# Moving the SBUF tiles of a float32r block kernel to addresses that are multiples of 512 bytes

## The chip, the core and the metric

The kernel runs on one core of a Trainium2 chip. The metric is the device time of one execution in microseconds (us). The numbers below come from three timed runs of the kernel before and from one further execution that was recorded with the hardware profiler.

## What is computed

One layer of a block over 2048 positions of width 1024, all in float32. Cut to what matters:

```python
h = rms_norm(x, norm_mix_g)
z = h @ w_in                                  # 1024 -> 2568 columns
u_a, v_a = gelu(z[:512]), gelu(z[512:1024])   # group A: gated heads over blocks of 128 positions
q, k, v, f_logit = the rest of z              # group B: 8 heads of 64, causal attention with a forget gate
out_a = u_a * (masked w_s @ layer_norm(v_a) + b_s)
out_b = softmax(q k^T / 8 + c[t] - c[s]) v    # c = cumsum(log_sigmoid(f_logit + f_bias)), s <= t
x = x + concat(out_a, out_b) @ w_out
a = rms_norm(x, norm_ffn_g) @ w_up            # 1024 -> 2 * 2816, then a causal convolution of width 3
x = x + (silu(gate) * value) @ w_down         # 2816 -> 1024
out = rms_norm(x, norm_final_g)
```

## The kernel before

**Three matmuls for one.** Each float32 operand of a large product is split into a high and a low part of type float32r, and each product is made of three matmuls: high by high, high by low, low by high (`mm3`, lines 208 to 212; `prod`, 1154 to 1156; `mms`, 1356). Nearly all matmuls have a 128x128 stationary operand and a moving operand of 512 columns, which is 2048 bytes in each partition.

**Stages, in order of time.** The input projections for keys, queries, values and the gated heads (`phase_a`, to about 590 us); the output projection of the first half of the tokens (`c_half`); the up-projection and convolution of the first half (`d_half`, from about 720 us to 1470 us); the output projection of the second half (`c_late`); its up-projection, done with seven half-size products instead of eight (`late_half`, `up_mms`); and the down-projection, done in the same way (`down`, from about 1990 us).

**What sets the order.** From about 120 us to 1490 us attention runs as a filler between the matmuls of the other stages: `tick` counts matmuls and calls `step`, which takes the next piece of the generator `b_stream`. A piece of `b_max` (lines 750 and 751) is one block of scores for the row maxima, a piece of `b_mix` has the scores again, transposed (811, 812), and the products with the values (799, 800). The matmul of line 750 uses 96 partitions, all others use 128. A scheduler then orders the instructions of each engine.

**Where tiles lie.** [...] The first pool, `const` (lines 215 to 225), holds the identity that transposes use, `mhalf`, `cols` and `halo`, and ends at byte 3872, which is 7 x 512 + 288. All pools of the left side follow, and since the tiles that large matmuls read have sizes that are multiples of 512 bytes, each of them begins at 288 bytes past a multiple of 512: `whi`, `wlo`, `thi`, `tlo`, `m1`, `t1`, `m2`, `t2`, `v`, `ph`, `pl`, `xh`, `xl`, `wh`, `wl` and the parts of the late stages. On the right side lies attention's pool `bpool`, opened by `b_open` and filled by `b_consts` (masks) and `b_max` (small statistics). To its left, from about 970 us to 1490 us, lies `bxpool`, opened in `d_half` (line 958 and after), from which `room` takes spare buffers for attention; their names have a plus: `e+`, `m2+`, `ph+`, `pl+`, `v+`. They begin at 96 bytes past a multiple of 512. In the built program 320 matmuls read a `+` tile as the moving or as the stationary operand.

**Small rings that the change touches.** `a_layernorm` takes three 64-byte tiles `lns` a call and `a_forget` takes eight 128-byte tiles `fs` a call (function `turn`, lines 597 to 613); `BUFS` says how many buffers each ring has.

Of the kernel before, what the change touches and what calls it, by code (L numbers as in the profile page):

```python
# [8 lines left out]
F32 = mybir.dt.float32  # L9
F32R = mybir.dt.float32r  # L10
BF16 = mybir.dt.bfloat16
AF = mybir.ActivationFunctionType
# [6 lines left out]
P = 128  # L19
# [19 lines left out]

BUFS = {  # L40
    "raw": 2, "rawl": 3, "whi": 5, "wlo": 5, "thi": 2, "tlo": 2, "acc": 4,
# [11 lines left out]
def f32(ap):  # L53
    return ap.bitcast(F32)
# [26 lines left out]
class Block:  # L81
# [134 lines left out]
    def constants(self):  # L216
        nc, a, tc = self.nc, self.a, self.tc
        cp = self.cpool = self.ctx.enter_context(tc.tile_pool(name="const", bufs=1))
        self.ident = cp.tile([P, P], F32, name="ident")
        make_identity(nc, self.ident)  # L220
        self.mhalf = cp.tile([P, 8], F32, name="mhalf")
        nc.gpsimd.memset(self.mhalf, -0.5)
        self.cols = cp.tile([P, 200], F32, name="cols")
        self.halo = cp.tile([P, 2 * NF, 2], F32, name="halo")
        nc.gpsimd.memset(self.halo, 0.0)
        dp = self.ctx.enter_context(tc.tile_pool(name="dram", bufs=1, space=DRAM))
        self.ones_d = dp.tile([2, HALF], F32, name="ones_d")
        t = lambda n, k, s: [dp.tile(s, F32, name=f"{n}{i}") for i in range(k)]
        self.qx = t("qx", 2, [8, 128, HALF])
        self.kx = t("kx", 2, [8, 132, HALF])  # L230
        self.cc = t("cc", 2, [8, 2, HALF])
        self.vd = t("vd", 2, [HALF, 8, P])
        self.mixh = t("mixh", 4, [D, TB])
        self.mixl = t("mixl", 4, [D, TB])
        self.rows_d = [t(f"rows{i}_", 8, [P, D]) for i in range(2)]
        self.act_d = [t(f"act{i}_", NF, [P, HALF]) for i in range(2)]
        self.tw_d = t("tw", NF // 2, [P, 2, D])
# [342 lines left out]
    def a_forget(self, half, b):  # L580

        nc, sp, pp = self.nc, self.sp, self.ap
        hT = self.hT[b]
        pl = self.til(pp, [16, TB], F32, "mm" if half else "tp")
        for k in range(KC):
            nc.tensor.matmul(pl, lhsT=self.wf[:, k, :], rhs=hT[0][:, k, :], start=k == 0, stop=False)
            self.tick()
            nc.tensor.matmul(pl, lhsT=self.wf[:, k, :], rhs=hT[1][:, k, :], start=False, stop=k == KC - 1)
            self.tick()
        lg = self.til(sp, [16, TB], F32, "ln")  # L590
        nc.scalar.activation(lg, pl, AF.Copy)

        def turn():
            pt = self.til(pp, [P, 4, 16], F32, "tp")
            for i in range(4):
                nc.tensor.transpose(pt[:, i, :], lg[:, i * P:(i + 1) * P], self.ident[:16, :16])
            t = lambda: self.til(sp, [P, 4, 8], F32, "fs")
            z0, z = t(), t()
            nc.vector.tensor_copy(z0, pt[:, :, 8:16])
            nc.vector.tensor_tensor(z, pt[:, :, 0:8], z0, op=ALU.add)  # L600
            nc.vector.tensor_tensor(z, z, self.scales[half][b].unsqueeze(2).broadcast_to([P, 4, 8]), op=ALU.mult)
            nc.vector.tensor_tensor(z, z, self.fb.unsqueeze(1).broadcast_to([P, 4, 8]), op=ALU.add)

            az, e, u, d, ru, lu = t(), t(), t(), t(), t(), t()
            nc.scalar.activation(az, z, AF.Abs)
            nc.scalar.activation(e, az, AF.Exp, scale=-1.0)
            nc.vector.tensor_scalar(u, e, 1.0, None, ALU.add)
            nc.vector.scalar_tensor_tensor(d, u, -1.0, e, op0=ALU.add, op1=ALU.subtract)
            nc.vector.reciprocal(ru, u)
            nc.vector.tensor_tensor(d, d, ru, op=ALU.mult)  # L610
            nc.scalar.activation(lu, u, AF.Ln)
            nc.vector.tensor_tensor(lu, lu, d, op=ALU.subtract)
            nc.vector.scalar_tensor_tensor(lu, z, 0.0, lu, op0=ALU.min, op1=ALU.subtract)
            lh = self.til(sp, [P, 4, 8], F32R, "fr")
            ll = self.til(sp, [P, 4, 8], F32R, "fr")
            nc.vector.tensor_copy(lh, lu)
            nc.vector.tensor_tensor(ll, lu, f32(lh), op=ALU.subtract)
            self.defer(70, lambda: cumulate(lh, ll))

        def cumulate(lh, ll):  # L620
            pc = self.til(pp, [8, TB], F32, "tp")
            for i in range(4):
                w, o = self.tri[:, 0:TB - P * i], pc[:, P * i:]
                nc.tensor.matmul(o, lhsT=lh[:, i, :], rhs=w, start=i == 0, stop=False)
                nc.tensor.matmul(o, lhsT=ll[:, i, :], rhs=w, start=False, stop=i == 3)
            c = self.til(sp, [8, TB], F32, "ln")
            nc.vector.tensor_scalar(c, pc, self.carry, None, ALU.add)
            nc.vector.tensor_copy(self.carry, c[:, TB - 1:TB])
            for sc, dst in ((-1.0, self.cc[half]), (1.0, self.kx[half][:, 130:132, :])):
                hl = self.til(sp, [8, 2, TB], F32R, "vn")  # L630
                rh, rl = hl[:, 0, :], hl[:, 1, :]
                nc.scalar.activation(rh, c, AF.Copy, scale=sc)
                nc.vector.scalar_tensor_tensor(rl, c, sc, f32(rh), op0=ALU.mult, op1=ALU.subtract)
                self.dma(dst[:, 0, b * TB:(b + 1) * TB], f32(rh))
                self.dma(dst[:, 1, b * TB:(b + 1) * TB], f32(rl))

        self.defer(12, turn)


# [10 lines left out]
    def b_consts(self):  # L650
        nc, bp = self.nc, self.bp
        ones = self.til(self.sp, [P, TB], F32, "st")[:2, :]
        nc.gpsimd.memset(ones, 1.0)
        for i in range(2):
            self.dma(self.ones_d[:, i * TB:(i + 1) * TB], ones)
        for k in self.kx:
            self.dma(k[:, 128:130, :], self.ones_d.unsqueeze(0).broadcast_to([8, 2, HALF]))
        self.mask = bp.tile([P, TB], BF16, name="mask")
        nc.gpsimd.memset(self.mask, 0.0)

        nc.gpsimd.affine_select(out=self.mask, in_=self.mask, compare_op=ALU.is_ge, fill=BIG, base=384,
                                pattern=[[-1, TB]], channel_multiplier=1)

        self.maskT = bp.tile([P, P], BF16, name="maskT")
        nc.gpsimd.memset(self.maskT, 0.0)
        nc.gpsimd.affine_select(out=self.maskT, in_=self.maskT, compare_op=ALU.is_ge, fill=BIG, base=0,
                                pattern=[[1, P]], channel_multiplier=-1)

        self.rowsel = bp.tile([8, 4, P], BF16, name="rowsel")
        nc.gpsimd.memset(self.rowsel, 1.0)  # L670
        for base, mult in ((0, 1), (1, -1)):
            nc.gpsimd.affine_select(out=self.rowsel, in_=self.rowsel, compare_op=ALU.is_ge, fill=0.0, base=base,
                                    pattern=[[-2 * mult, 4], [0, P]], channel_multiplier=mult)
        self.M1, self.T1 = [[self.til(self.mp, [P, TB], F32R, tag) for _ in range(2)] for tag in ("m1", "t1")]
        for m in self.M1:
            nc.gpsimd.memset(f32(m[64:128, :]), 0.0)
            nc.gpsimd.memset(f32(m[96:104, :]), 1.0)
        for t in self.T1:
            nc.gpsimd.memset(f32(t[64:128, :]), 0.0)
            self.dma(f32(t[66:68, :]), self.ones_d[:, 0:TB])  # L680
# [835 lines left out]
```

## Time and profile before

| | before |
|---|---|
| median of 3 runs | 2429.42 us (2428.42 to 2429.88) |
| the profiled execution, its own time | 2425.31 us |
| its span, first to last instruction | 2423.6 us |
| TensorE (PE) busy | 2404.0 us, 99% |
| weight loads (PEld) busy | 1981.1 us, 82% |
| VectorE (DVE) busy | 1755.0 us, 72% |
| ScalarE (ACT) busy | 1352.4 us, 56% |
| GpSimd (POOL) busy | 315.8 us, 13% |
| granted TensorE clock, mean | 0.999 |

In the rows of the profile, PE is a matmul and PEld a weight load. A row of groups names the line of the kernel, the engine, the operation, output<-inputs, sizes and the count, then the busy time in us and the mean duration in ns, then idle time of the engine ahead of them. A row of the timeline begins with the start and the length in us. Matmuls overlap in the pipeline: the recorded length of one of 512 columns is 0.39 us, but the next one starts about 0.23 us after it, so the cost of a matmul is the distance between two starts, and a longer recorded length shows a longer distance.

### The profile page before, as it was taken

What the parts mean: (1) busy time and instruction counts of PE and PEld (TensorE: products, weight loads), DVE (VectorE), ACT (ScalarE), POOL (GpSimd) and SP (SyncE); (2) the same over time, 40 slices, a digit from 0 to 9 for tenths busy, and PEclk for the clock granted to TensorE, in tenths of its full rate; (3) what the DMA queues carried; (4) which work ended last, traced back from release to release, by engine and by line L of the source; (5) the groups of instructions that cost most, each with busy time, mean ns of one, the idle gap of its engine ahead of it and who ended that gap; (6) DMA issues with size and microseconds to landing.
All of it is one profiled execution on the core that took longest, in us unless ns stands there. A gap on an engine that the chain in (4) does not pass through costs nothing.

```text
span 2423.6 us, 32604 instructions
## 1 busy us (share of the span) xinstructions
PE 2404.0 (99%) x10984; PEld 1981.1 (82%) x10984; DVE 1755.0 (72%) x3086; ACT 1352.4 (56%) x2635; POOL 315.8 (13%) x303
## 2 busy tenths in 40 slices
PE   9999999999999999999999999999999999999998
PEld 7788888788788888888888888888888888888887
DVE  5448785565568778878778775598888877957776
ACT  4347766554446555766776764365555455454443
POOL 3114140000241221111012101100000000000000
PEclk9999999999999999999999999999999999999999
DMA  8854636658855444555445565312222238538633
GB/s 291 276 142 120 202 114 178 170 169 265 261 188 183 160 163 161 163 170 181 149 154 180 165 190 199 130 52 88 86 79 87 85 95 306 164 99 296 207 118 122
DMA packets 245031, 400.51 MB, mean 165 GB/s; under 512 B 51240, under 2 KB 109736, under 8 KB 243440
## 3 DMA queue, kind: packets, MB, share of 16 engines
q1 hardware_dynamic: 239824, 374.31, 48.7%
q0 software_dynamic: 5040, 24.12, 2.6%
q8 instruction: 87, 1.43, 0.2%
q14 instruction: 80, 0.66, 0.1%
HBM read 304.76 MB, written 93.72 MB: 164 GB/s over the span
## 4 chain that ended last, share of the span: by engine, by line
PE 68%; DMA 2%; DVE 2%; ACT 1%; issue 1%; POOL 0%; SPq 0%; DVEq 0%; POOLq 0%; ACTq 0%
PE D L1356 14%; PE mm L212 8%; PE mm L208 8%; PE mm L210 8%; PE A L1154 3%; PE A L1156 3%; PE A L1155 3%; PE o L800 2%; PE o L799 2%; PE B L1156 2%; PE B L1155 2%; PE B L1154 2%; PE s L751 1%; PE s L750 1%; PE s L812 1%; PE s L811 1%
## 5 line engine op out<-in xcount | busy, mean ns | idle before, releaser
L210 PE MATMUL mm<-tlo,whi 128*128 128x512 f32 x912 | 358.3, 393 | 0.0
L212 PE MATMUL mm<-thi,wlo 128*128 128x512 f32 x912 | 357.5, 392 | 0.0
L208 PE MATMUL mm<-thi,whi 128*128 128x512 f32 x912 | 357.2, 392 | 0.0
L150 POOL TENSOR_SCALAR whi<-raw 128x1024 fp32r<-128x1024 f32 (+1 forms) x112 | 128.2, 1146 | 980.5 <-PE mm L210 576.5
L208 PE MATMUL mm<-whi,thi 128*128 128x512 f32 x640 | 252.0, 395 | 0.7 <-POOL whi L150 0.7
L212 PE MATMUL mm<-whi,tlo 128*128 128x512 f32 x640 | 251.5, 394 | 1.1 <-DMA tlo<-mixl 1.1
L210 PE MATMUL mm<-wlo,thi 128*128 128x512 f32 x640 | 251.1, 393 | 0.2
L759 ACT ACTIVATE s<-s,part 128x512 f32<-128x512 f32 (+3 forms) x261 | 154.6, 592 | 141.8 <-DVE part L754 85.2
L823 DVE TENSOR_TENSOR pl<-e,ph 128x512 fp32r<-128x512 f32 (+1 forms) x218 | 146.6, 681 | 76.0 <-ACT ph L822 42.4
L208 PEld LDWEIGHTS mm<-thi,whi 128*128 128x128 f32 x912 | 171.4, 188 | 35.9
L212 PEld LDWEIGHTS mm<-thi,wlo 128*128 128x128 f32 x912 | 171.5, 188 | 34.9
L210 PEld LDWEIGHTS mm<-tlo,whi 128*128 128x128 f32 x912 | 171.5, 188 | 34.9
L817 ACT ACTIVATE e<-s 128x512 f32<-128x512 f32 (+1 forms) x222 | 113.8, 529 | 109.5 <-DVE s L815 49.5
L162 DVE TENSOR_TENSOR wlo<-raw,whi 128x1024 fp32r<-128x1024 f32 x104 | 135.6, 1304 | 51.0 <-POOL whi L150 50.8
L822 ACT ACTIVATE ph<-e 128x512 fp32r<-128x512 f32 (+1 forms) x218 | 120.1, 563 | 43.6 <-PE o L799 41.1
L1356 PE MATMUL D<-wl,xh 128*128 128x512 f32 x368 | 141.4, 389 | 0.0
L1356 PE MATMUL D<-wh,xh 128*128 128x512 f32 x368 | 140.8, 389 | 0.2 <-DVE xo L1434 0.2
L212 PEld LDWEIGHTS mm<-whi,tlo 128*128 128x128 f32 x640 | 120.3, 188 | 24.7 <-DMA tlo<-mixl 1.4
L208 PEld LDWEIGHTS mm<-whi,thi 128*128 128x128 f32 x640 | 120.3, 188 | 24.3 <-POOL whi L150 1.0
L210 PEld LDWEIGHTS mm<-wlo,thi 128*128 128x128 f32 x640 | 120.3, 188 | 24.1 <-DVE wlo L162 1.0
L1356 PE MATMUL D<-wh,xl 128*128 128x512 f32 x368 | 137.2, 389 | 0.0
L754 DVE TENSOR_REDUCE part<-s 128x1 f32<-128x512 f32 x149 | 98.5, 683 | 26.6 <-PE s L751 25.9
(1860 smaller groups left out, 5834.8 us busy)
## 6 DMA issues: line engine op xcount, KB each, us to landing
raw<-in_w_up_dram SPq DMA_DIRECT2D x72, 512.0 KB
m<-kx SPq DMA_DIRECT2D x134, 256.0 KB
m<-kx SPq DMA_DIRECT2D x160, 136.0 KB
x<-act SPq DMA_DIRECT2D x84, 256.0 KB
raw<-in_w_in_dram SPq DMA_DIRECT2D x36, 512.0 KB
v<-vd SPq DMA_DIRECT2D x67, 256.0 KB
raw<-in_w_out_dram SPq DMA_DIRECT2D x24, 512.0 KB
tw<-in_w_down_dram SPq DMA_DIRECT2D x11, 1024.0 KB
```

The source lines that it names most:

```text
L150: self.cast_ins = self.nc.gpsimd.tensor_scalar(out, in_, 1.0, 0.0, ALU.mult, ALU.add).ins
L162: nc.vector.tensor_tensor(lo, raw, f32(hi), op=ALU.subtract)
L208: mm(ps, lhsT=ah[k], rhs=bh[k], start=k == 0, stop=False)
L210: mm(ps, lhsT=ah[k], rhs=bl[k], start=False, stop=False)
L212: self.last_mm = mm(ps, lhsT=al[k], rhs=bh[k], start=False, stop=k == n - 1).ins
L759: nc.scalar.activation(ps[:, :n], ps[:, :n], AF.Exp, scale=-1.0, bias=dst, accum_out=ls[:, tt, sb:sb + 1])
L822: nc.scalar.activation(ph[:, c], e[:, c], AF.Copy)
L823: nc.vector.tensor_tensor(pl[:, c], e[:, c], f32(ph[:, c]), op=ALU.subtract)
L1154: mm(ps, lhsT=xh[:, ks], rhs=yh[:, k, :], start=fresh and k == 0, stop=False, **kw)
L1155: mm(ps, lhsT=xh[:, ks], rhs=yl[:, k, :], start=False, stop=False, **kw)
L1156: mm(ps, lhsT=xl[:, ks], rhs=yh[:, k, :], start=False, stop=k == 3, **kw)
L1356: nc.tensor.matmul(bank[t], lhsT=x[i][:, ts], rhs=w[k], start=fresh and j == 0 and i + k == 0, stop=last and i == 1, **kw)
```

## The change

An unused tile of 224 bytes in a partition is put at the end of the `const` pool, and one of 96 bytes behind `maskT` in attention's pool. Everything in the left pools moves up by 224 bytes, so that the tiles that were at 288 are now at a multiple of 512; the tiles of `bxpool` move down by 96 bytes, from 96 past a multiple to a multiple. To make room, the ring `lns` has 8 buffers instead of 9 and the ring `fs` 7 instead of 9, and `a_forget` takes seven tiles a call: the absolute value and the exponential are written in place.

```diff
-    "x": 4, "st": 4, "ln": 2, "vn": 4, "u": 2, "lns": 9, "fs": 9, "fr": 3,
+    "x": 4, "st": 4, "ln": 2, "vn": 4, "u": 2, "lns": 8, "fs": 7, "fr": 3,
...
         self.halo = cp.tile([P, 2 * NF, 2], F32, name="halo")
+        cp.tile([P, 56], F32, name="even")
...
-            az, e, u, d, ru, lu = t(), t(), t(), t(), t(), t()
-            nc.scalar.activation(az, z, AF.Abs)
-            nc.scalar.activation(e, az, AF.Exp, scale=-1.0)
+            e, u, d, ru, lu = t(), t(), t(), t(), t()
+            nc.scalar.activation(e, z, AF.Abs)
+            nc.scalar.activation(e, e, AF.Exp, scale=-1.0)
...
         self.maskT = bp.tile([P, P], BF16, name="maskT")
+        bp.tile([P, 24], F32, name="even")
```

Not all that matmuls read comes to a multiple of 512. The identity stays at 128 past one, the ring `e` of attention (written and read by ScalarE and VectorE, not by matmuls) stays at 288, `tri` (moving operand of 32 matmuls in `cumulate`, lines 624 and 625) moves from 448 to 160, and `sw` (stationary in `a_mixed`) from 480 to 448. The sequence of instructions on each of the five engines is the same in both programs apart from the names of buffers; six instructions of GpSimd (three of line 570, three of line 150) differ in whether they also wait for an earlier instruction of GpSimd itself.

## The prediction

> **What bounds the kernel now.** I read the page first: the span and the engines' busy time, then the chain that ended last by engine.
>
> ```profile
> span 2423.6 us, 32604 instructions
> PE 2404.0 (99%) x10984; PEld 1981.1 (82%) x10984; DVE 1755.0 (72%) x3086; ACT 1352.4 (56%) x2635; POOL 315.8 (13%) x303
> PE 68%; DMA 2%; DVE 2%; ACT 1%; issue 1%; POOL 0%; SPq 0%; DVEq 0%; POOLq 0%; ACTq 0%
> ```
>
> TensorE is busy all the time and no other engine is near it. Only the distance between two matmul starts can move the end, by each matmul's own share. Next I read those distances. First the stretch of the second half's up-projection (busy time by windows; columns: length, PE busy and number of matmuls, clock, DMA), with three rows of its timeline:
>
> ```profile
> 1600.00:1990.00 390.00, 390.00 (x1722) 1.00 0.25 83
> ...
> 1700.17 0.39 PE L1155 MATMUL A<-tlo,xsP3h 128*128 128x512 f32 x1
> 1700.40 0.39 PE L1156 MATMUL A<-tlo,xsP3l 128*128 128x512 f32 x1
> 1700.62 0.39 PE L1154 MATMUL A<-tlo,xsP3h 128*128 128x512 f32 x1
> ```
>
> 390 us for 1722 matmuls of 512 columns is 226.5 ns each, without variation. All these operands lie at 288 past a multiple of 512. I call this the steady spacing. Then the groups, where the recorded length tells the spacing: 389 ns in the late stages, more in the early ones, where attention runs between (last columns: busy us, mean ns of one).
>
> ```profile
> L1356 PE MATMUL D<-wl,xh 128*128 128x512 f32 x368 | 141.4, 389 | 0.0
> ...
> L210 PE MATMUL mm<-tlo,whi 128*128 128x512 f32 x912 | 358.3, 393 | 0.0
> L212 PE MATMUL mm<-thi,wlo 128*128 128x512 f32 x912 | 357.5, 392 | 0.0
> L208 PE MATMUL mm<-thi,whi 128*128 128x512 f32 x912 | 357.2, 392 | 0.0
> L208 PE MATMUL mm<-whi,thi 128*128 128x512 f32 x640 | 252.0, 395 | 0.7 <-POOL whi L150 0.7
> L212 PE MATMUL mm<-whi,tlo 128*128 128x512 f32 x640 | 251.5, 394 | 1.1 <-DMA tlo<-mixl 1.1
> L210 PE MATMUL mm<-wlo,thi 128*128 128x512 f32 x640 | 251.1, 393 | 0.2
> ...
> L750 PE MATMUL s<-m,t 96*128 96x512 f32 x178 | 68.4, 403 | 1.9 <-DMA t<-qx 1.2 <-DMA t<-cc 0.7
> L751 PE MATMUL s<-m,t 128*128 128x512 f32 x157 | 59.2, 401 | 0.0
> ```
>
> So there are two losses to look at: the excess over the steady spacing in the early stages, and the steady spacing itself.
>
> **What starts an excess.** The timeline shows the steady stream broken by a matmul that differs from the one before it. Here it is one with 96 partitions (its sizes begin with 96):
>
> ```profile
> 1009.09 0.39 PE L208 MATMUL mm<-thi,whi 128*128 128x512 f32 x1
> 1009.32 0.40 PE L750 MATMUL s<-m,t 96*128 96x512 f32 x1
> 1009.55 0.40 PE L751 MATMUL s<-m,t 128*128 128x512 f32 x1
> 1009.79 0.40 PE L210 MATMUL mm<-tlo,whi 128*128 128x512 f32 x1
> ```
>
> And here two that read `+` tiles, at 96 past a multiple of 512 between tiles at 288:
>
> ```profile
> 1126.27 0.40 PE L799 MATMUL o<-ph+_2355_10034,v 128*128 128x512 f32 x1
> 1126.51 0.40 PE L208 MATMUL mm<-thi,whi 128*128 128x512 f32 x1
> 1126.75 0.39 PE L800 MATMUL o<-pl+_2356_10035,v 128*128 128x512 f32 x1
> 1126.98 0.39 PE L210 MATMUL mm<-tlo,whi 128*128 128x512 f32 x1
> ...
> 1127.91 0.39 PE L212 MATMUL mm<-thi,wlo 128*128 128x512 f32 x1
> ```
>
> From the first of these rows to the last there are seven spacings in 1.64 us, 234 ns each. So a start that differs from its neighbours' does cost something: about 8 ns on the matmul and on a few behind it.
>
> **The change part by part.** The order of instructions stays, so every term is a duration.
>
> *The `+` tiles come to the same start as the rest.* This is the term that I count on. 320 matmuls read a `+` tile. The lower bound is 0: in that stage matmuls with 96 partitions and transposes break the stream as well, and followers may pay on their account anyway. The upper bound is the whole run above: seven spacings of 234 against 226.5 are 53 ns for two such matmuls, 26 ns each, times 320 is 8.4 us. I take one excess of 7.5 ns for each, 320 x 7.5 = 2.4 us, because the rows with 96 partitions show the same excess right beside them, and what a follower pays is then no longer the tile's doing. [...]
>
> *All other tiles go from 288 to 0 together.* Their starts relative to each other stay as they are. The steady spacing is the same whichever of the tiles is read, and the one float32r operand that starts elsewhere and is not a `+` tile, `tri` at 448 (a multiple of 64), shows no better one:
>
> ```profile
> 492.59 0.40 PE L624 MATMUL tp<-tri,fr 128*8 128x512 f32 x1
> 492.82 0.39 PE L625 MATMUL tp<-tri,fr 128*8 128x512 f32 x1
> 493.05 0.22 PE L811 MATMUL s<-t,m 128*128 128x128 f32 x1
> ```
>
> Two spacings of 0.23 us. I take 0 for this term; what it would be otherwise is the first rival.
>
> *Smaller rings.* The next user of `fs` comes long after the last reader, 59.37 against 72.85 us, and with 8 buffers of `lns` the third call's last tile (written from 205.67 us) takes the one that the first call read last at 174.87 us:
>
> ```profile
> 59.19 0.18 DVE L617 TENSOR_TENSOR fr<-fs,fr 128x32 fp32r<-128x32 f32 x1
> 72.85 0.18 DVE L599 COPY fs<-tp 128x32 f32<-128x32 f32 x1
> ...
> 173.65 1.22 DVE L562 TENSOR_TENSOR ln<-ln,lns 128x1024 f32<-128x1024 f32 x1
> ...
> 205.67 2.90 POOL L570 TENSOR_TENSOR lns<-lns,mhalf 128x16 f32<-128x16 f32 x1 [7.14 <-PE s L784]
> ```
>
> Covers of 13 and 31 us, cost 0; without the cover, a wait of the small chain in `a_forget`, whose product is used 70 matmuls later. Three more casts on GpSimd wait for an earlier instruction of GpSimd, which runs in order anyway: 0. *VectorE, ScalarE and DMA* also see other starts. VectorE is busy for 72% and ScalarE for 56% of the span, and 2%, 1% and 2% of the chain that ended last are VectorE, ScalarE and DMA, so a few per cent of one of them is under 1 us: 0.
>
> The sum: the profiled execution took 2425.3 us (span 2423.6 and 1.7 around it), minus 2.4 is 2422.9. It was 4.1 us faster than the median of the runs shown, so the median to expect is 2429.4 - 2.4 = 2427.0 us, 0.1% less. A measurement of this kernel can tell about 0.2%, or 4.9 us, from no change, so this is no change.
>
> **The rivals.**
>
> *First: the steady spacing is itself a loss from the start at 288, and goes.* For it speak two kinds of short matmul, four transposes that read the identity (at 128 past a multiple of 512) and twelve rows of the gate's products that read `vn` (at 288):
>
> ```profile
> 236.58 0.60 PE L183 MATMUL tp<-ident,u 128*128 128x128 f32 x4
> ...
> 225.16 1.50 PE L524 MATMUL tp<-vn,sw 128*128 128x128 f32 x12
> ...
> L524 PE MATMUL tp<-vn,sw 128*128 128x128 f32 x128 | 18.3, 275 | 0.0
> L183 PE MATMUL tp<-ident,u 128*128 128x128 f32 x64 | 10.3, 272 | 0.0
> ```
>
> Their spacings are (0.60 - 0.272)/3 = 109 and (1.50 - 0.275)/11 = 111.4 ns: with 288 it is 1.9% slower. On 2404 us of TensorE that is 46 us, and the time 2383. Against it: `tri`, and that `vn` is read in two pieces there and the identity in one. [...] Chance 0.14.
>
> *Second: every excess of the early stages goes,* because a stream that starts on a multiple of 512 finds its steady spacing again at once. From the groups: 912 x (4 + 3 + 3) + 640 x (6 + 5 + 4) ns are 18.7 us, 178 x 14 + 157 x 12 another 4.4, together 23 us; the recorded means contain true waits too, so I take 14, and 2415 us. Against it: 96 partitions and transposes still break the stream. Chance 0.16.
>
> *Third, slower: the steady spacing is a property of the start 288 and does not hold at 0.* Place: the late stages from 1570 us, which hold it now. Price: there are (2420 - 1570)/0.2265 = 3750 matmuls; with the 6 ns that the `whi` rows have over 389 it is 22 us, hence 2449 us. It decides from 1200 matmuls on (the 2.4 us gained and 4.9 more, at 6 ns). For it speaks only that a change of start is seen at all; against it, that the steady spacing is the same for all tiles and whatever the other engines do. Chance 0.08.
>
> **How the numbers follow.** Forecast 0.62: 2427.0 us, on its own 2421 (the upper bound of the first term) to 2432. Faster by over 0.2% are the first two rivals, 0.30; slower the third, 0.08; within 0.2% 0.62. The range of 8 in 10 takes the second rival in, with the upper bound of the first term against its middle value, to 2411, and a quarter of the third, to 2436; outside lie the first rival, 0.14, and most of the third, 0.06.
>
> **What would show it.** Right: the window 1600 to 1990 again holds about 1722 matmuls, and rows around a `+` tile start 0.23 us apart, while those of line 750 stay at 0.40 us. Wrong: 389 ns in the late groups gives way to another number (first or third rival), or the `mm` groups fall to 389 in the early stages (second).

## The result, and the profile after

| | before | after |
|---|---|---|
| median of 7 runs each, in turn on one chip | 2429.42 us (2427.00 to 2430.46) | 2421.35 us (2419.37 to 2422.35) |
| ratio after to before, 95% interval | | 0.997 (0.9959 to 0.9980) |
| the profiled execution, its own time | 2425.31 us | 2421.7 us |

By the medians the change makes the kernel 8.1 us faster, 0.33%; by the ratio it is 0.30%. The predicted 2427.0 us has the right sign and the range holds the result, but the likeliest case, "within 0.2%", did not come: a gain of 2.4 us was forecast. The two profiled executions differ by only 3.6 us. So there were two things to find out: where the other 5 us come from, and why the profiles show only part of the gain.

The page of the changed kernel, its span, the busy times, and the chain that ended last by engine:

```profile
span 2420.0 us, 32601 instructions
PE 2401.1 (99%) x10984; PEld 1980.9 (82%) x10984; DVE 1757.0 (73%) x3086; ACT 1352.3 (56%) x2635; POOL 315.2 (13%) x303
PE 93%; DMA 2%; DVE 2%; ACT 1%; issue 1%; POOL 0%; SPq 0%; DVEq 0%; POOLq 0%; ACTq 0%
```

VectorE and ScalarE do their work in the same time as before (1755.0 and 1352.4 us).

TensorE's share of the chain, 93% against 68%, is not more work (busy for 2401.1 against 2404.0 us). The shares of the kernel before add up to 74% only, because its chain can be followed back no further than to a wait of TensorE for `op`:

```profile
632.20 0.61 DVE op L835
632.85 0.50 PE o L799
```

The chain of the changed kernel goes back to the first transfers. This wait is the last of three that are told of below.

The late up-projection, by windows as before (length, PE busy and matmuls, weight loads, the other engines, clock, share of the DMA engines, GB/s):

```profile
1600.00:1990.00 390.00, 390.00 (x1723) 322.92 (x1722) 330.48 (x414) 203.02 (x308) 0.59 (x1) 1.00 0.25 83
```

1723 matmuls against 1722: the steady spacing did not move. Nor did the short matmuls that read `vn`, which begins on a multiple of 512 now; twelve of them take 1.50 us as before:

```profile
224.90 1.50 PE L525 MATMUL tp<-vn,sw 128*128 128x128 f32 x12
```

The timeline around two matmuls that read `+` tiles, and around one with 96 partitions (lines 752 and 753 here are 750 and 751 before):

```profile
1124.15 0.39 PE L801 MATMUL o<-ph+_2351_10032,v 128*128 128x512 f32 x1
1124.38 0.39 PE L208 MATMUL mm<-thi,whi 128*128 128x512 f32 x1
1124.60 0.39 PE L802 MATMUL o<-pl+_2352_10033,v 128*128 128x512 f32 x1
1124.83 0.39 PE L210 MATMUL mm<-tlo,whi 128*128 128x512 f32 x1
...
1125.74 0.39 PE L212 MATMUL mm<-thi,wlo 128*128 128x512 f32 x1
```

```profile
1007.62 0.40 PE L752 MATMUL s<-m,t 96*128 96x512 f32 x1
1007.85 0.40 PE L753 MATMUL s<-m,t 128*128 128x512 f32 x1
1008.09 0.40 PE L210 MATMUL mm<-tlo,whi 128*128 128x512 f32 x1
```

Seven spacings from the first `+` row to the last take 1.59 us, 227 ns each; before they took 1.64 us. All rows there are back at 0.39 us. The rows with 96 partitions stay at 0.40 us. In the groups, the `mm` rows that run beside attention moved by 0 to 1 ns and did not reach 389:

```profile
L210 PE MATMUL mm<-tlo,whi 128*128 128x512 f32 x912 | 357.9, 392 | 0.0
L208 PE MATMUL mm<-thi,whi 128*128 128x512 f32 x912 | 356.8, 391 | 0.0
...
L752 PE MATMUL s<-m,t 96*128 96x512 f32 x178 | 68.3, 403 | 1.6 <-DMA t<-qx 0.9 <-DMA t<-cc 0.5 <-issue 0.2
```

To add up small differences I took the distance from each matmul's start to the next one's, and from it the steady spacing of its width (226.67 ns for 512 columns). What is left I call **excess** when it is up to 20 ns, and a **long wait** at those matmuls where at least one kernel has over 120 ns (what lies between differs little). Summed over the kernel, the excess fell from 15.8 to 12.9 us, so 2.9 us, near the forecast; the long waits were 9.8 us and 9.2 us. The size of the fall is known to some tenths: over matmuls of 256 and more columns alone it is 2.4 us. Counted so, the stretch from 970 to 1490 us, where `+` tiles are read, has 7.3 us of excess before and 4.6 after, and in every other stage the two kernels agree within 0.1 us. The rest of the gain is not in these two traces.

### The profile page after: what moved, and what is told of

The parts are those of the page before. It is cut to its first block, busy times and chain, and to the rows that moved or that the text cites. A ratio compares the mean times of both kernels' runs of the same rounds, so it can differ in the third digit from the quotient of the medians.

```text
span 2420.0 us, 32601 instructions
## 1 busy us (share of the span) xinstructions
PE 2401.1 (99%) x10984; PEld 1980.9 (82%) x10984; DVE 1757.0 (73%) x3086; ACT 1352.3 (56%) x2635; POOL 315.2 (13%) x303
## 4 chain that ended last, share of the span: by engine, by line
PE 93%; DMA 2%; DVE 2%; ACT 1%; issue 1%; POOL 0%; SPq 0%; DVEq 0%; POOLq 0%; ACTq 0%
PE D L1358 15%; PE mm L212 14%; PE mm L210 14%; PE mm L208 14%; PE A L1156 3%; PE A L1157 3%; PE A L1158 3%; PE o L802 2%; PE o L801 2%; PE s L753 2%; PE s L752 2%; PE s L814 2%; PE s L813 2%; PE B L1157 2%; PE B L1158 2%; PE B L1156 2%
```

## The experiments

Two theories stood at the start. Theory R: only a difference of start between neighbouring matmuls' operands costs time. Theory A: a start on a multiple of 512 is itself what helps. A third, N, was that the first profile of before was a lucky execution. The numbers of all kernels are in one table, worked out from the traces: the start of left tiles that matmuls read and of `+` tiles, modulo 512; the sum of excess and of long waits in us; of these the three waits between 627 and 634 us, which are told of below; the share of 2048-byte DMA packets that took over 100 ns between 640 and 950 us; and the time against the kernel before, timed in turn on the same chip (its medians there: 2427.79, 2427.68 and 2428.56 us). The ratio compares runs taken in turn; it differs from the quotient of the two medians by up to 0.07%.

```
kernel    left  +    excess  long   near   packets  median   ratio (95% interval)
                             waits  628    >100 ns
before    288   96   15.8     9.8   1.7    0.20     2429.42
before2   288   96   15.6    13.5   2.2    0.19     2428.42  1.0005 (0.9996 to 1.0014)
rings     288   96   15.7    12.9   1.6    0.19     2427.30  1.0001 (0.9992 to 1.0009)
right     288    0   15.4    11.7   1.7    0.19     2427.11  0.9999 (0.9990 to 1.0008)
left        0   96   15.6     7.5   0.0    0.13     2423.34  0.9984 (0.9975 to 0.9993)
match288  288  288   13.1    12.3   2.0    0.18     2425.07  0.9986 (0.9977 to 0.9995)
all64      64   64   13.5     9.4   0.7    0.18     2425.14  0.9990 (0.9981 to 0.9998)
after       0    0   12.9     9.2   0.0    0.14     2421.35  0.9970 (0.9959 to 0.9980)
after2      0    0   12.8     7.4   0.0    0.14     2420.37  0.9977 (0.9966 to 0.9987)
k128        0    0    9.0    13.2   1.4    0.13     2418.08  0.9962 (0.9949 to 0.9976)
raw0      288   96   15.1     9.3   1.3    0.17     2425.85  0.9991 (0.9982 to 1.0000)
raw288      0    0   13.5     6.5   0.0    0.11     2420.43  0.9971 (0.9960 to 0.9982)
plus352   288  352   15.7    12.1   2.0    0.19     one run
plus32    288   32   13.0     8.4   1.9    0.19     one run
```

The waits are distances from start to start, and so a little longer than the idle times in the rows below. In `match288` and `all64`, 1.4 and 1.6 us are left out of them that lie in stretches with a lower granted clock (mean 0.75 from 664.5 to 668.5 us, and 0.60 from 8 to 11 us). Edits are shown against the changed kernel. The expectations for `right` and `all64` speak of a theory D, which came from the first four experiments and is told further below.

**The kernel before, once more** (`before2`, as it was).

> The kernel before, unchanged, for a second profile and more times. In the two traces so far the spans differ by 3.6 us, the medians by 8.1: the profiled execution of before (2425.3 us) lies below all of its timed runs (2427.0 to 2430.5). Theory R (a mismatch of start between the operands of neighbouring matmuls costs time, nothing else in this change does): the span of this second profile lies near 2424 again and the small excess of matmuls over their steady spacing sums to about 16 us again; then 4 us of the gain lie in something that comes and goes from run to run. Theory N (the first profile of before was lucky): the span comes out at 2426 to 2429 us, and the added time shows as waits for transfers or as more excess. Time against the kernel before: ratio 1.000.

The page's span, and the waits of TensorE between 600 and 640 us (us in total, times, longest):

```profile
span 2427.5 us, 32604 instructions
```

```profile
PE mm L208 <- POOL whi L150: 1.1, 1, 1.1
PE o L799 <- DVE op L835: 0.6, 1, 0.6
PE s L812 <- DMA m<-kx: 0.2, 1, 0.2
```

The span is 3.9 us longer than in the first profile of before; the excess is the same (15.6 us) and the long waits are 3.7 us more. Theory N held: the first profiled execution had fewer waits than most, which is also why it lay 4.1 us under the median.

**The smaller rings alone** (`rings`).

```diff
-        cp.tile([P, 56], F32, name="even")
...
-        bp.tile([P, 24], F32, name="even")
```

> Only the smaller rings of lns and fs and the absolute value and exponential in place; all tiles keep the starts of before (288, and 96 for the + tiles). Theory R and theory A (a start on a multiple of 512 is itself what helps) both: 2429 us, ratio 1.000. Rival: the waits that went near 630 us in the changed kernel went because of the rings and not because of the starts; then about 1.5 us less than before, and the 0.65 us wait for the cast at 627.8 us is absent from this trace too.

Ratio 1.0001, and the waits near 628 us are there (1.6 us). The rings cost and bring nothing that shows here.

**One of the two spaces alone** (`left`: only the one behind the constants; `right`: only the one in attention's pool).

```diff
-        bp.tile([P, 24], F32, name="even")
```

> The rings and the space behind the constants, but none in attention's pool: all tiles that the stationary side reads start at 0, the + tiles stay at 96, so the mismatch between neighbours stays (96 against 0). Theory R: as before, 2427 to 2430 us, ratio 0.999 to 1.000; matmuls with + tiles keep a mean excess of about 5 ns. Theory A: most of the gain is there, 2422 to 2424, ratio 0.997 to 0.998.

```diff
-        cp.tile([P, 56], F32, name="even")
```

> Only the space in attention's pool (and the rings): + tiles at 0, all tiles of the left side at 288 as before. Theory D: the starts still differ and the transfers are those of before, so 2427 to 2428 us, ratio 0.9995 to 1.000; the excess of matmuls with + tiles stays at about 5 ns, the waits near 628 us are there. Theory A (a start on a multiple of 512 is what helps a matmul): the excess of the + tiles falls, 2425, ratio 0.999.

Neither theory was right on `left`. Its excess is that of before (15.6 us; matmuls with `ph+` and `v` keep 6.4 ns against 6.6), as theory R says, and still it gains 0.16%. `right` gains nothing (0.9999; excess 15.4 us): bringing `+` tiles to a multiple of 512 did not help them while the others were at 288.

**Equal starts that are no multiples of 512** (`match288`, `all64`).

```diff
-        cp.tile([P, 56], F32, name="even")
...
-        bp.tile([P, 24], F32, name="even")
+        bp.tile([P, 80], F32, name="even")
```

> The rings, no space behind the constants, and 80 numbers (320 bytes) of space in attention's pool: all tiles start at 288 past a multiple of 512, the + tiles too; nothing starts on a multiple of 512. Theory R: as fast as the changed kernel, 2421 to 2422 us, ratio 0.997; the excess of matmuls with + tiles falls to 0 to 1.5 ns. Theory A: 2427 to 2430 us, ratio 0.999 to 1.000.

```diff
-        cp.tile([P, 56], F32, name="even")
+        cp.tile([P, 72], F32, name="even")
...
-        bp.tile([P, 24], F32, name="even")
+        bp.tile([P, 8], F32, name="even")
```

> All tiles, the + tiles too, start at 64 past a multiple of 512. Equal starts: by theory D the excess is 12.9 to 13.1 us in all, as in the changed kernel. For the transfers it tells whether a multiple of 64 bytes is enough: if so 2421 us, ratio 0.997, no waits near 628 us and packets as short as in the changed kernel (a mean of 28.1 ns for 512 bytes against 29.0); if it takes a multiple of 512, 2424 to 2425 us, ratio 0.9986, and the waits are there.

The timeline of `match288`, then of `left`, at the same matmuls:

```profile
1129.44 0.39 PE L800 MATMUL o<-ph+_2351_10031,v 128*128 128x512 f32 x1
1129.67 0.39 PE L208 MATMUL mm<-thi,whi 128*128 128x512 f32 x1
1129.90 0.39 PE L801 MATMUL o<-pl+_2352_10032,v 128*128 128x512 f32 x1
...
1131.03 0.39 PE L212 MATMUL mm<-thi,wlo 128*128 128x512 f32 x1
```

```profile
1123.20 0.40 PE L800 MATMUL o<-ph+_2351_10031,v 128*128 128x512 f32 x1
1123.43 0.39 PE L208 MATMUL mm<-thi,whi 128*128 128x512 f32 x1
1123.66 0.40 PE L801 MATMUL o<-pl+_2352_10032,v 128*128 128x512 f32 x1
...
1124.82 0.40 PE L212 MATMUL mm<-thi,wlo 128*128 128x512 f32 x1
```

1.59 us at 288 and 288, 1.62 us at 0 and 96. So the matmuls' part goes by theory R: equal starts were enough here, at 0 or at 288. It is worth 2.4 to 2.9 us of excess, and `match288` measures 0.14%; that it would have the whole gain, 0.997, as theory R said, was wrong. The other part comes with the left side's start, 0.16% in `left`. The two add up to the changed kernel's 0.30%, each known to about 0.1%.

`all64` lies between: 0.9990. Its excess, 13.5 us, is a little more than expected (matmuls with `ph+` and `v` keep 2.3 ns, against 1.5 in `match288`). Of the three waits near 628 us one is left (0.7 us), and long packets are nearly as frequent as at 288 (0.18).

**What the left side's start brings.** In the table it is the long waits: the seven kernels with those tiles at 288 (without `raw0`, below) have 8.4 to 13.5 us, mean 11.5, and the four at 0 (without `k128`) 6.5 to 9.2, mean 7.6. Single executions vary by 2 to 3 us, but three waits do not: they are there in all with tiles at 288, `raw0` too, and in none of these four. Of the difference of 3.9 us between the means, 2.1 lie between 600 and 640 us, in these three waits and in small ones just ahead of them. The rest is spread over later waits, in which kernels with equal starts differ among themselves by more than that. GpSimd's casts of the weights show what they wait for (start and length; in brackets idle time and what ended it), here in `before2` and then in the changed kernel:

```profile
617.19 1.41 POOL L150 TENSOR_SCALAR whi<-raw 128x1024 fp32r<-128x1024 f32 x1 [0.90 <-PE mm L212]
627.52 1.05 POOL L150 TENSOR_SCALAR whi<-raw 128x1024 fp32r<-128x1024 f32 x1 [8.92 <-PE s L812]
628.85 1.89 POOL L150 TENSOR_SCALAR whi<-raw 128x1024 fp32r<-128x1024 f32 x1 [0.28 <-DMA raw<-in_w_out_dram]
```

```profile
617.33 1.41 POOL L150 TENSOR_SCALAR whi<-raw 128x1024 fp32r<-128x1024 f32 x1 [0.90 <-PE mm L212]
624.20 1.05 POOL L150 TENSOR_SCALAR whi<-raw 128x1024 fp32r<-128x1024 f32 x1 [5.46 <-DMA raw<-in_w_out_dram]
625.44 1.99 POOL L150 TENSOR_SCALAR whi<-raw 128x1024 fp32r<-128x1024 f32 x1 [0.19 <-DMA raw<-in_w_out_dram]
```

The casts before these start within 0.2 us of each other, then the weights land 3.3 us earlier and TensorE, which needs the cast at 628 us and waited 1.1 us for it in `before2`, no longer waits. (The cast at 627.52 us is put down to a matmul. In the first profile of before the same cast is put down to one too; there the last piece of the weights lands at 626.54 us and the cast starts at 626.71 us, so it follows the landing.) The way from there to TensorE's second wait, 0.6 us, is VectorE's `wlo` behind the casts (628.60 and 631.80 us) and `op` behind that (632.94 us). Meanwhile the DMA engines are busy with a queue of other transfers. By windows, between 604 and 616 and between 616 and 627 us (last two columns: share of the DMA engines, GB/s), `before2`, then the changed kernel:

```profile
604.00:616.00 12.00, 12.00 (x57) 10.09 (x56) 5.65 (x13) 4.57 (x10) 0.77 (x1) 1.00 1.01 383
616.00:627.00 11.00, 10.81 (x49) 8.65 (x49) 4.57 (x5) 3.52 (x7) 1.70 (x2) 1.00 0.97 236
```

```profile
604.00:616.00 12.00, 12.00 (x58) 10.05 (x57) 4.87 (x10) 4.71 (x10) 0.62 (x1) 1.00 1.03 381
616.00:627.00 11.00, 11.00 (x52) 9.19 (x52) 6.34 (x7) 3.52 (x7) 4.46 (x4) 1.00 0.74 209
```

They are busy all the time until 616 us in both (1.01 and 1.03); after that they are at 0.97 in `before2`, and at 0.74 after the change, which has less left to move. Up to 616 us both move the same (383 and 381 GB/s); the lead comes from before, 277 against 232 GB/s between 597 and 604 us, in this pair of executions. Theory D was formed from this: the second part is transfers that take less time.

**The changed kernel once more** (`after2`, no edit).

> The changed kernel again, as the mark for its neighbours in this group. The group before gave two parts that add up: tiles of the left side alone 0.9984, equal starts alone 0.9986. Theory D (two parts: equal starts of neighbouring matmuls, about 2.7 us of excess; and transfers to and from tiles that start on an even address, which takes 1.7 to 2.2 us of waits near 628 us): 0.997, no wait over 0.1 us between 627 and 634 us, excess of the matmuls 12.9 us in all. Rival (the waits near 628 us come and go by chance): the waits are here this time.

Ratio 0.9977, and the three waits are absent again, so the rival of chance did not hold. The two timings of the change give 0.30 and 0.23%.

**Which tiles' transfers** (`raw0`: `raw`, `acc`, `x`, `vn` at 0 and the tiles that attention and the projections read at 288; `raw288`: the reverse, with the `+` tiles at 0). Spaces of 288 and 224 bytes are put behind `rawp` and `wpool` (224 and 288 in `raw288`), the small rings shortened further. The tiles of the late stages (`xh`, `wh` and others) go with `raw`; the table has the start of the others.

```diff
         self.rawp = self.rest.enter_context(tc.tile_pool(name="rawp", bufs=1))
+        self.rest.enter_context(tc.tile_pool(name="gap1", bufs=1)).tile([P, 72], F32, name="gap1")
...
         self.wpool = es.enter_context(tc.tile_pool(name="wpool", bufs=1))
+        es.enter_context(tc.tile_pool(name="gap2", bufs=1)).tile([P, 56], F32, name="gap2")
...
-        bp.tile([P, 24], F32, name="even")
```

> Only tiles that no matmul of the waiting stretch reads start on a multiple of 512: raw (the weights as they are loaded), acc and x, and vn; the casts and all operands that attention's and the projections' matmuls share stay at 288, the + tiles at 96. Theory D, with the transfers into and out of these tiles as the ones that count: the waits near 628 and 633 us go or shrink to under 0.3 us in all, waits of over 0.12 us sum to 7 to 9 us instead of 12 to 13, excess of the matmuls 15.6 as before, time 2423 to 2425 us, ratio 0.9985. Rival: what counts are the transfers into the tiles that matmuls read (thi, tlo, keys, queries and values: 5 MB of the 8 MB that move between 597 and 628 us); then the waits stay, and 2427 to 2428 us, ratio 1.000.

```diff
-        cp.tile([P, 56], F32, name="even")
...
+        self.rest.enter_context(tc.tile_pool(name="gap1", bufs=1)).tile([P, 56], F32, name="gap1")
...
+        es.enter_context(tc.tile_pool(name="gap2", bufs=1)).tile([P, 72], F32, name="gap2")
```

> The other way round: raw, acc, x and vn start at 288, all tiles that attention's and the projections' matmuls share at 0, the + tiles too. The excess of the matmuls is that of the changed kernel, 12.9 us, by every theory. If the transfers of raw, acc and vn count: waits near 628 us as in the kernel before, 2424 to 2425 us, ratio 0.9987. If those into the matmuls' tiles count: no such waits, 2420 to 2421 us, ratio 0.997.

GpSimd's casts and TensorE's waits in `raw0`, then the casts in `raw288`, where no wait of TensorE is left between 600 and 640 us:

```profile
617.86 1.41 POOL L150 TENSOR_SCALAR whi<-raw 128x1024 fp32r<-128x1024 f32 x1 [0.90 <-PE mm L212]
626.77 1.05 POOL L150 TENSOR_SCALAR whi<-raw 128x1024 fp32r<-128x1024 f32 x1 [7.50 <-PE s L813]
```

```profile
PE o L800 <- DVE op L836: 0.6, 1, 0.6
PE mm L208 <- POOL whi L150: 0.2, 1, 0.2
```

```profile
618.62 1.41 POOL L150 TENSOR_SCALAR whi<-raw 128x1024 fp32r<-128x1024 f32 x1 [0.91 <-PE mm L212]
625.96 1.05 POOL L150 TENSOR_SCALAR whi<-raw 128x1024 fp32r<-128x1024 f32 x1 [5.92 <-DMA raw<-in_w_out_dram]
```

My reading of theory D, that the transfers of `raw` and `acc` count, fell for the waits near 628 us; its rival held there. `raw288` is as fast as the changed kernel, 0.9971, with `raw` and `acc` at 288. `raw0` gains at most a little (its interval reaches 1.0000), and the waits stay; its 0.9991 lies between the two forecasts, so a small share of `raw` and `acc` is not ruled out. What counts is the start of the other group. In it are the tiles that are written by transfers and read by matmuls: `thi`, `tlo`, keys, queries, values. Tiles that engines write (`whi`, `wlo`, `ph`, `pl`) moved with them and were not tried apart. That it is the transfers rests on the packets. Of those with 2048 bytes, 11 to 14% take over 100 ns between 640 and 950 us in the five kernels with those tiles at 0, and 17 to 20% in all others, `all64` and `raw0` among them. In the late stages, where `raw0` has its tiles at 0 and `raw288` at 288, the 80th percentile is 84 ns in the first and 86 in the second, as it is 84 in the other kernels at 0, and 85 or 86 in those at 288 and 64.

The runs do not show why the start counts for a packet, nor why every fifth packet instead of every eighth takes over 100 ns while attention runs.

**How equal starts must be** (`plus352`, `plus32`; left side at 288).

```diff
-        cp.tile([P, 56], F32, name="even")
...
-        bp.tile([P, 24], F32, name="even")
+        bp.tile([P, 64], F32, name="even")
```

> One look at the rule of the matmuls: left side at 288, + tiles at 352, so they differ by 64 bytes instead of 192. If starts count by the 64 bytes, 352 is as good as 288: the mean excess of matmuls that read a + tile and v falls from 5 to 6.6 ns to about 1 to 1.5. If they count by 512 or 128 bytes, it stays at 5 to 6.6 ns. Read from the trace alone.

In `plus32` the last line has 16 instead of 64.

> The same with a difference of 256 bytes: left side at 288, + tiles at 32. If starts count by 256 bytes, the mean excess of matmuls that read a + tile and v falls to 1 to 1.5 ns; if by 512, it stays at 5 to 6.6 ns. Read from the trace alone.

The timeline of `plus352`, then of `plus32`:

```profile
1128.39 0.40 PE L800 MATMUL o<-ph+_2351_10031,v 128*128 128x512 f32 x1
1128.63 0.40 PE L208 MATMUL mm<-thi,whi 128*128 128x512 f32 x1
1128.87 0.39 PE L801 MATMUL o<-pl+_2352_10032,v 128*128 128x512 f32 x1
```

```profile
1124.05 0.39 PE L800 MATMUL o<-ph+_2351_10031,v 128*128 128x512 f32 x1
1124.28 0.39 PE L208 MATMUL mm<-thi,whi 128*128 128x512 f32 x1
1124.51 0.39 PE L801 MATMUL o<-pl+_2352_10032,v 128*128 128x512 f32 x1
```

The mean excess of matmuls with `ph+` and `v` is 6.6 ns at a difference of 64 bytes, 6.4 at 96, 6.6 at 192, 7.0 at 288; it is 1.4 at 256 and 1.5 at 0 (2.3 in `all64`). So in these kernels starts that are equal modulo 256 bytes were enough, and equal modulo 64 was not. Whether equal modulo 128 would do is open: a difference of 128 was not tried.

**The next thing that breaks the stream** (`k128`: the changed kernel with 128 partitions in the maximum's matmul).

```diff
+        nc.gpsimd.memset(f32(t1[96:104, :]), 0.0)
...
-                nc.tensor.matmul(ps[:, :n], lhsT=t1[0:96, ts], rhs=m1[0:96, :n], start=True, stop=False)
+                nc.tensor.matmul(ps[:, :n], lhsT=t1[0:128, ts], rhs=m1[0:128, :n], start=True, stop=False)
```

> The changed kernel with the matmuls of attention's maximum over 128 partitions instead of 96 (the 8 words of t1 that are added per row's partitions are set to 0, so the sum is the same). It asks whether a different number of partitions is the next thing that breaks the steady stream. Theory: the 280 matmuls with 96 partitions lose their 6.3 ns each and their followers as much again, 3 to 4 us in all, so 2417 to 2418 us, ratio 0.9955. Rival (the excess is the price of changing between accumulations, whatever the number of partitions): 2421 us, ratio 0.997, the excess of this line stays.

Its rows of that matmul and the next, and TensorE's waits between 600 and 640 us:

```profile
1009.60 0.39 PE L753 MATMUL s<-m,t 128*128 128x512 f32 x1
1009.82 0.39 PE L754 MATMUL s<-m,t 128*128 128x512 f32 x1
```

```profile
PE o L802 <- DVE op L838: 0.5, 1, 0.5
PE mm L208 <- POOL whi L150: 0.2, 1, 0.2
```

And GpSimd's casts there:

```profile
617.97 1.48 POOL L150 TENSOR_SCALAR whi<-raw 128x1024 fp32r<-128x1024 f32 x1 [0.84 <-PE mm L212]
627.01 1.05 POOL L150 TENSOR_SCALAR whi<-raw 128x1024 fp32r<-128x1024 f32 x1 [7.56 <-PE s L815]
```

The theory of the excess held: 12.8 us became 9.0, as expected. The time followed by 2.3 us only (2418.08 against 2420.37 us), and the intervals of the two overlap. The profiled execution, 2422.72 us, is the slowest of the five, so its trace does not show the median's gain. In it the waits near 628 us are there again (1.4 us) with all tiles at 0: TensorE is no earlier than in the changed kernel (the cast that a matmul releases starts at 617.97 against 617.33 us), and the weights land 2.8 us later. So a start at 0 alone does not keep these waits away. The edit also adds an instruction on GpSimd, the engine of the casts, and the order of some matmuls differs; what delays the weights here is not known. `k128` has the lowest median of all kernels here, but that it beats the changed kernel is not shown.

## Why the prediction was right in sign and too small

- **The `+` tiles: right in the sum, by luck in its make-up.** Forecast 2.4 us; the excess fell by 2.4 to 2.9 us in the changed kernel (15.1 to 15.8 us in kernels with unequal starts, 12.8 to 13.5 with equal ones). I had read the excess "on the matmul and on a few behind it" and then charged each of the 320 matmuls with 7.5 ns and those behind with nothing. Between 970 and 1490 us the 320 matmuls lost only 0.8 us, 2.4 ns each. In the group `ph+` by `v` the mean went from 6.6 to 1.5 ns, in `pl+` by `v` from 5.1 to 0.9; but in the group with `m2+` as the stationary operand, which comes behind a matmul with 96 partitions, it rose from 6.7 to 9.5. The other 1.9 us came off the matmuls behind.
- **All other tiles from 288 to 0: right for the matmuls.** `left` has the excess of before (15.6 us), and the steady spacing stayed (1723 matmuls in the window of 390 us, 1722 before).
- **The rings: right,** 1.0001.
- **VectorE, ScalarE and DMA: the step that failed.** I wrote that a few per cent of an engine with 2% of the chain is under 1 us, and took 0. For VectorE and ScalarE their busy times give no sign against it. For the transfers it was wrong by about 4 us: `left` measures 0.16%, and long waits fell from 11.5 to 7.6 us on average, of which 2.1 us are there each time. The chain did not lead to it: before, it could be followed back only to 632 us, to the last of the three waits that went, and the longer chain after has the same 2% of DMA. The fault was to scale the wait. The wait here was the small difference between two long times, the row of transfers ahead of it and TensorE's own work. In `before2` 23 us of full queues (DMA share 1.01 and 0.97 from 604 to 627 us) ended 1.1 us after TensorE needed the weights; in `raw288` and the changed kernel they end 1.6 and 3.3 us earlier (casts at 625.96 and 624.20 instead of 627.52 us), and the whole wait goes.
- **From the profile to the median: right as a rule, not explained then.** The first profile's 4.1 us under the median were waits that the execution happened not to have. So the difference of the two first profiles hides most of the second part. That the result, 2421.35 us, lies at the lower end of the forecast's own range, 2421, is luck too: this end stood for 8.4 us from the `+` tiles alone.
- **Rivals.** The steady spacing is the same, 226.67 ns (first and third rival out), and 12.9 us of excess remain (second out). The rows of `vn` that spoke for the first were no sign of the start: they kept their 1.50 us. None of the rivals had transfers in it.

What stays open: how packets that are shorter by 2 ns become 3 us at the landing of the weights; whether the packets grow long by their own start alone or because matmuls read the same tiles meanwhile, since no kernel moved one without the other; and where the last 2 to 3 of the 8.1 us lie, since the later waits vary too much between single executions to tell.

## What to carry to other kernels

In a float32r stream like this one let operands of neighbouring matmuls begin at the same place modulo 256 bytes: here a pool that is stacked from the other end (`side="right"`), 64 to 288 bytes off, cost 5 to 7 ns in most matmuls of 512 columns that read it (1.4 ns at a difference of 256), and in sum more than that in those behind (1.9 against 0.8 us); this was 0.1% of the time. Let tiles that transfers fill and matmuls read begin on a multiple of 512 (64 was not enough, with 18% of the packets over 100 ns; 256 was not tried). With TensorE busy for 99% of the span this was worth a few waits, 0.16% in `left`, not a share of the transfers, and in `k128` the waits near 628 us were there with all tiles at 0. And where a change is worth 0.3%, profile both kernels twice: the waits of two executions of one kernel differed by half of that (9.8 and 13.5 us).

## What the runs showed of the hardware

- The steady spacing of a float32r matmul of 512 columns was 226.67 ns with all tiles of the left side at 288 past a multiple of 512 (before) and at 0 (after), in the window from 1600 to 1990 us; at 64 (`all64`) the excess over it sums to 13.5 us in the whole kernel, against 12.9 after.
- A matmul of 512 columns over 96 partitions among those over 128 had a mean excess of 6.9 ns before and 6.5 after, and the one behind it in the same piece (line 751, 753 after) 7.7 and 8.0; with 128 partitions (`k128`), zeros in the added rows, both have a recorded length of 0.39 us, and the kernel's excess fell by 3.8 us, from 12.8 to 9.0.
- In the changed kernel fewer packets of 2048 bytes took over 100 ns while attention ran (14% against 19 to 20%), with transfers to and from tiles at 0 in place of 288 past a multiple of 512; at 64 they were 18%.
